# Rearranged places at the two ends of an expert loop: the overflow branch behind the first gathers, rows, norm factors and first weights in other buffers

## The chip, the cores and the metric

The kernel runs on one core of a Trainium2 chip. The metric is the device time of one execution in microseconds (us); smaller is better. The core has a matrix engine (PE, with its weight loads shown as PEld), a vector engine (DVE), a scalar engine (ACT), a general engine (POOL) and a queue engine (SP) that only issues DMAs here. Each works through its own list of instructions in order; they meet through semaphores, and each DMA queue is fed in the order in which its engine reaches the issuing instruction.

## What is computed

Two transformer blocks on 512 tokens of width 1024, in 32-bit floats. The first block ends with a mixture of 64 experts, and its layer norm; the second begins with an RMS norm and a projection.

```python
def first_block(...):                 # mixer, cross-attention, then
    ff = moe_ffn(x, w_router, router_bias, w_exp_gu, w_exp_down, w_sh_gu, w_sh_down)
    x = layer_norm(DEEPNORM_ALPHA * x + ff, ln3_g, ln3_b)
    return x

def moe_ffn(x2d, ...):                # each token goes to 8 of 64 experts, weights w
    ...
    out = swiglu(x2d[tok], w_exp_gu[e], w_exp_down[e]) * w      # summed into the token's row
    return routed + swiglu(x2d, w_sh_gu, w_sh_down)             # plus a shared expert

def second_block(x, norm_mix_w, w_in, ...):
    h = rmsnorm(x, norm_mix_w)
    z = h @ w_in
    ...
```

## The kernel before, in words

**Products.** Every float matrix is split into a rounded part and a remainder (`hi`, `lo`: line 118 on ACT, line 119 on DVE or, where asked for, POOL), and a product is three matmuls (`mm3`, lines 176 to 178).

**Places.** Tiles come from pools. A pool closed and another opened at the same addresses share memory, tile by tile: the later tile's first writer waits for the last user of whatever lay there. The left and the right side of memory are two stacks. In the expert stage the right side holds 32 KB of expert weights (`whl1`, slots 2 and 3 of `wtiles`) and then a ring of 7 raw weight places of 8 KB (`wraw`); the left side holds four `xt` places, a pool `mc` (with the gather buffers `gx[0]` to `gx[2]`), another 32 KB of expert weights (`whl0`, slots 0 and 1) and the loop's small tiles. The second block puts its transposed input `hT` where `whl1` was, its weight pool `w3` (3 raw places, 4 pairs of hi and lo, `wvg`) where `wraw` was, and on the left the big tiles `oB0`, `oB1`, `QSa`, `QSb`, `KH`, `KL` and a pool `nrm`.

**Order.** The order on each engine is fixed at build time by a planner that takes the instructions by priority (their order in the text) as its own estimate of the times finds them ready. So an instruction may be moved ahead of others that stand before it in the text. `issue_after(ins)` puts what is in its block behind `ins` on `ins`'s engine. A branch (`tc.If`, line 1363) is one unit on every engine: nothing is moved into it, but work is placed on either side of it.

**The start of the expert stage** (`moe`, from line 1396). `slot_steps` (lines 1250 to 1281) turns the router's choice into the list of rows of each expert, for four experts at a time: one-hot compares on DVE, small matmuls into the bank `lg`, casts on DVE. `load(i)` issues the three raw weight loads of expert i (3 MB). `moe_overflow` (line 1355) handles experts with more than 96 rows in a branch that is skipped here: each engine loads the largest count into a register (line 1362) and branches. It names two slots of `wtiles`, two `xt` places, one raw place and `gx[0]`. Then `fetch(i)` gathers the rows of expert i into `gx[i % 3]` by an indirect DMA on POOL (line 1287), `weights(i)` splits its weights and issues `load(i + 2)`, `rows(i)` transposes the gathered rows (line 1296) and splits them to `gT`, and `gated(i)` multiplies. `wtiles` hands out four slots in turn; the shared expert's weights are in slots 0 to 2. The branch takes slots 3 and 0, expert 0 slots 1 and 2.

**The end of the expert stage.** Each expert's result rows are scattered to a table in memory with 8 slots a token (plus one for the shared expert), except for the last two experts, whose rows are held and added by one-hot matmuls (line 1576). After the loop the first weights of the next block are loaded into freed expert weight places (`pre`, lines 1532 to 1535). The table is read back, per token tile t (128 tokens): `x3[t]` (slot 8) and four parts `(t, j)` of 1 MB, two slots each. Six parts of tiles 0 and 1, and later two more, go to the raw ring (`ring`); DVE adds some (`add_v`, line 1585), PE adds others through identity matmuls (`add_t`, lines 1595 and 1598). `ln3` loads the norm's factors `ln3g`, `ln3b` (line 257), reads the parts of tiles 2 and 3, and gives the functions for the norm.

**The start of the second block** (`block2`, line 1723). `begin` splits the first weights from `pre` into `w3` (ACT and POOL). `normed(t)` is the layer norm and the RMS norm of tile t (ACT 283, DVE 288 and 289, ACT 1648, DVE 1651 giving `hn`); for t = 0 it is queued behind `cast`, the last split on ACT. The loop over t transposes `hn` (line 299), multiplies by the two first weights, and behind tile 1 adds the rows of tiles 2 and 3 (`rows_v` on DVE, `rows_t` on PE).

Of the kernel before, what the change touches and what calls it, by code (L numbers as in the profile page):

```python
# [53 lines left out]
class Net:  # L54
# [1228 lines left out]
    def gather(self, gx, idx, pool, x2d, bufs=2):  # L1283
# [6 lines left out]
        gT = [pool.tile([P, KD, C], R, tag=f"gT{i}", name=self.name("gT"), bufs=bufs) for i in range(2)]  # L1290

        def turn(*halves):
# [62 lines left out]
    def moe_overflow(self, rk, vals, cnt, iota, gx, table, x2d, wge, wde):  # L1355

        nc, tc = self.nc, self.tc
        C = self.CAP
        wgu = [self.wtiles(4, 512) for _ in range(2)]
        wdn = [self.xt().rearrange("p (c n) -> p c n", c=2) for _ in range(2)]  # L1360
        raw = self.wrp.tile([P, self.RCH], F, tag="raw", name=self.name("raw"), bufs=self.nraw)
        most = nc.values_load(cnt[0:1, 64:65], min_val=0, max_val=S)
        with tc.If(most > C):
            with tc.For_i(0, 64, 1) as i:
                with tc.tile_pool(name="ov", bufs=1) as op_:
# [10 lines left out]
                    for b in range(1, -(-S // C)):  # L1376
# [4 lines left out]
                        gT = self.gather(gx, idx, op_, x2d, 1)()  # L1381
                        self.scatter(self.turn_rows(self.gated(gT, wgu, op_), op_), row, w, wdn, table, gx)

    def moe(self, x2, xT, lg):
# [75 lines left out]
        load(0)  # L1460
        load(1)
        self.moe_overflow(rk, vals, cnt, iota, gx[0], table, x2d[:, :], wge, wde)
        ep_s, ep = self.pool("ex")

# [4 lines left out]
        def fetch(i):  # L1469
            if i < E:  # L1470
                turn[i] = self.gather(gx[i % 3], sel(i)[0], ep, x2d[:, :])

        def rows(i, *halves):
            if i < E:
                gTs[i] = turn[i](*halves)
# [9 lines left out]

        fetch(0)
        fetch(1)
        weights(0)
        rows(0)
# [46 lines left out]
        y = self.wrp.tile([P, 2 * D], R, tag="raw", name=self.name("y"), bufs=self.nraw)  # L1536
        held[E - 2] = self.gx(1, R, C), self.gx(2, R, C)
        held[E - 1] = y[:C, :D], y[:C, D:]
# [7 lines left out]
        ring = lambda: self.wrp.tile([P, self.RCH], F, tag="raw", name=self.name("row"), bufs=self.nraw)  # L1546
        for t in range(2):
            nc.sync.dma_start(x3[:, t], self.table[t * P:(t + 1) * P, 8])
            for j in ((4, 6, 0, 2) if t == 0 else (0, 2)):
                read(t, j, ring())  # L1550
            if t == 0:
                for u in (2, 3):
                    nc.sync.dma_start(x3[:, u], self.table[u * P:(u + 1) * P, 8])
        turned(E - 2)
        back(E - 2)
        sgs[E - 1] = self.gated(gTs.pop(E - 1), wgs.pop(E - 1), ep)
# [10 lines left out]
        for j in (4, 6):  # L1567
            read(1, j, ring())
# [545 lines left out]
```

## Time and profile before

| | before |
|---|---|
| median of 3 runs | 2040.82 us (2033.28 to 2041.1) |
| the profiled execution, its own time | 2029.93 us |
| span of the profile | 2027.9 us |
| PE, DVE, ACT, POOL busy, share of the span | 91%, 68%, 51%, 24% |
| expert loop, first to last full pass | 615 to 1248 us |
| first matmul of the second block | 1325 us |

The profiled execution's own time is 2.0 us over its span, and 10.9 us under the median of the runs. Times in the rows below are microseconds from the start of the span. A row of a timeline gives start, duration, engine, line, operation, what it writes and reads, how often, and in brackets how long the engine stood idle before it and what released it. PE's busy time includes pipelining, so a PE that is busy all of a stretch is near, not at, its limit.

### The profile page before, as it was taken

The numbers are of one execution on the slowest core, as the hardware profiler recorded it, in microseconds if no ns is written. First come the engines' busy times: TensorE is split into PE (matmuls) and PEld (weight loads), VectorE is DVE, ScalarE is ACT, GpSimd is POOL, SyncE is SP. The second block draws the span as 40 slices with busy tenths as digits, with TensorE's granted clock in tenths as the row PEclk, the third lists the DMA queues.
The fourth block names the chain that finished last, engine by engine and source line by source line (L and its number), as shares of the span: only waits on it lengthen the run. The fifth ranks groups of instructions, "written<-read, shape, count | busy, mean of one in ns | idle before, by whom it ended". The sixth has DMA issues, their size and how long they took to land. (4 is left out here: it accounts for less than half of the span.)

```text
span 2027.9 us, 25347 instructions
## 1 busy us (share of the span) xinstructions
PE 1835.7 (91%) x9051; PEld 1407.0 (69%) x9051; DVE 1385.8 (68%) x2427; ACT 1037.6 (51%) x1522; POOL 483.4 (24%) x463
## 2 busy tenths in 40 slices
PE   6699899898979999998999898569999789999998
PEld 6477677686756776666766666248767578888886
DVE  8966677678788989887988887475576573333333
ACT  3363555336227878777877786124466542222220
POOL 6733111210432233432333442310033310000000
PEclk8899999899989999999999999789999899999999
DMA  5233323744339999999999998724210243333311
GB/s 144 63 85 104 115 63 117 246 154 143 146 142 340 365 356 361 351 350 339 365 359 362 350 359 293 292 111 128 65 53 1 84 125 95 102 94 95 103 52 42
DMA packets 178682, 381.00 MB, mean 188 GB/s; under 512 B 19749, under 2 KB 115313, under 8 KB 151929
## 3 DMA queue, kind: packets, MB, share of 16 engines
q1 hardware_dynamic: 156912, 327.54, 47.6%
q0 software_dynamic: 18784, 48.31, 7.0%
q10 hardware_dynamic: 2856, 3.49, 0.6%
q8 instruction: 73, 1.20, 0.2%
q14 instruction: 57, 0.46, 0.1%
HBM read 354.61 MB, written 41.16 MB: 195 GB/s over the span
## 5 line engine op out<-in xcount | busy, mean ns | idle before, releaser
L119 DVE TENSOR_TENSOR wlo<-raw,whi 128x1024 fp32r<-128x1024 f32 (+3 forms) x281 | 478.5, 1707 | 208.2 <-ACT whi L118 199.5
L118 ACT CAST whi<-raw 128x1024 fp32r<-128x1024 f32 (+3 forms) x288 | 406.2, 1415 | 407.6 <-PE acc L177 195.0
L177 PE MATMUL acc<-wlo,gT 128*96 128x512 f32 x512 | 207.5, 405 | 22.7 <-DVE wlo L119 22.3
L176 PE MATMUL acc<-whi,gT 128*96 128x512 f32 x512 | 215.9, 422 | 1.5 <-ACT whi L118 1.4
L1352 POOL DMA_INDIRECT table<-y,rowi x62 | 131.9, 2127 | 357.6 <-ACT aT L118 90.3
L178 PE MATMUL acc<-whi,gT 128*96 128x512 f32 x512 | 203.3, 397 | 0.0
L119 DVE TENSOR_TENSOR xt<-raw,xt 128x2048 fp32r<-128x2048 f32 x64 | 146.4, 2287 | 22.3 <-ACT xt L118 21.4
L176 PE MATMUL acc<-h3T,whi 128*128 128x512 f32 (+2 forms) x368 | 140.5, 382 | 0.2 <-ACT h3T L118 0.2
L177 PE MATMUL acc<-h3T,whi 128*128 128x512 f32 (+2 forms) x368 | 140.4, 382 | 0.1
L178 PE MATMUL acc<-h3T,wlo 128*128 128x512 f32 (+2 forms) x368 | 140.5, 382 | 0.0
L118 ACT CAST xt<-raw 128x2048 fp32r<-128x2048 f32 x64 | 122.1, 1908 | 14.7 <-DMA raw<-in_w_exp_down_dram 7.7
L177 PEld LDWEIGHTS acc<-wlo,gT 128*96 128x96 f32 x512 | 84.5, 165 | 55.0 <-DVE wlo L119 34.1
L1287 POOL DMA_INDIRECT gx<-x2d,idx x64 | 92.3, 1442 | 83.5 <-PE tr L1296 54.8
L178 PEld LDWEIGHTS acc<-whi,gT 128*96 128x96 f32 x512 | 83.7, 163 | 32.8 <-DVE gT L119 0.3
L176 PEld LDWEIGHTS acc<-whi,gT 128*96 128x96 f32 x512 | 85.8, 168 | 24.5 <-ACT whi L118 2.4
L176 PE MATMUL acc<-xt,aT 128*96 128x512 f32 x256 | 101.4, 396 | 1.0 <-ACT aT L118 1.0
L178 PE MATMUL acc<-xt,aT 128*96 128x512 f32 x256 | 100.6, 394 | 1.7 <-DVE aT L119 1.5
L177 PE MATMUL acc<-xt,aT 128*96 128x512 f32 x256 | 101.2, 395 | 0.0
L1349 ACT ACTIVATE y<-acc,wsl 96x512 f32<-96x512 f32 x124 | 83.6, 680 | 7.4 <-PE acc L178 7.1
L118 ACT CAST gT<-tr 128x384 fp32r<-128x384 f32 x128 | 59.7, 477 | 37.8 <-PE tr L1296 31.1
L176 PEld LDWEIGHTS acc<-h3T,whi 128*128 128x128 f32 x368 | 69.1, 188 | 13.8 <-ACT h3T L118 0.7
L177 PEld LDWEIGHTS acc<-h3T,whi 128*128 128x128 f32 x368 | 69.1, 188 | 13.6 <-DVE h3T L119 0.4
(718 smaller groups left out, 4427.3 us busy)
## 6 DMA issues: line engine op xcount, KB each, us to landing
raw<-in_w_exp_gu_dram SPq DMA_DIRECT2D x128, 1024.0 KB, 18.6
raw<-in_w_exp_down_dram SPq DMA_DIRECT2D x64, 1024.0 KB, 18.5
raw<-in_w_in_dram SPq DMA_DIRECT2D x36, 512.0 KB, 4.3
raw<-in_w_gate_dram SPq DMA_DIRECT2D x22, 512.0 KB, 4.0
raw<-in_w_up_dram SPq DMA_DIRECT2D x22, 512.0 KB, 3.8
raw<-in_w_down_dram SPq DMA_DIRECT2D x22, 512.0 KB, 3.7
row<-table SPq DMA_DIRECT2D x8, 1024.0 KB, 11.7
gsp<-sg POOLq DMA_DIRECT2D x16, 256.0 KB, 2.4
```

The lines of the kernel that those rows point to most:

```text
L118: first = nc.scalar.copy(hi, src)
L119: return first, (eng or nc.vector).tensor_tensor(lo, src, hi.bitcast(F), op=OP.subtract)
L176: mm(out, l[0], r[0], start=start, stop=False)
L177: mm(out, l[0], r[1], start=False, stop=False)
L178: mm(out, l[1], r[0], start=False, stop=stop)
L1287: nc.gpsimd.indirect_dma_start(out=gx, out_offset=None, in_=x2d, in_offset=bass.IndirectOffsetOnAxis(ap=idx, axis=0), bounds_check=S - 1, ...
L1349: nc.scalar.activation(y[:, nb * 512:(nb + 1) * 512], ps, AF.Copy, scale=w)
L1352: nc.gpsimd.indirect_dma_start(out=table, out_offset=bass.IndirectOffsetOnAxis(ap=row, axis=0), in_=y, in_offset=None, bounds_check=S * se ...
```

## The change

It has two parts.

At the start of the stage the order in the text is now: loads of experts 0 and 1, gathers of experts 0 and 1, the places of the branch, the split of expert 0's weights, the branch, and the rest. The branch uses `gx[2]` in place of `gx[0]`. Expert 0's weights take slots 3 and 0, the branch slots 1 and 2, which `self.wslot -= 2` hands to expert 1 again. The tiles `gT` are named when rows are transposed, not when they are gathered.

At the end of the stage the parts of tiles 0 and 1 are no longer read into the raw ring. Three go to the last expert's weight places (`spare`), the fourth of which holds the last expert's rows `y`; others go to `xt` places, and `(1, 6)` to a place of the second block. The reads stand behind `gated` of the last expert in the text. DVE adds one part more of tile 1, PE one less. The three rows of factors (`ln3_g`, `ln3_b`, `norm_mix_w`) go to the three raw places of `w3`, loaded before `begin`, where they were in the pool `nrm`, which now has an 8 KB place `row` for a part. The norm of tile 0 is no longer queued behind `cast`.

```diff
-        gT = [pool.tile([P, KD, C], R, tag=f"gT{i}", name=self.name("gT"), bufs=bufs) for i in range(2)]
-
-        def turn(*halves):
+        gT = []
+
+        def turn(pool, bufs, *halves):
+            if not gT:
+                gT.extend(pool.tile([P, KD, C], R, tag=f"gT{i}", name=self.name("gT"), bufs=bufs) for i in range(2))
...
         wgu = [self.wtiles(4, 512) for _ in range(2)]
-        wdn = [self.xt().rearrange("p (c n) -> p c n", c=2) for _ in range(2)]
-        raw = self.wrp.tile([P, self.RCH], F, tag="raw", name=self.name("raw"), bufs=self.nraw)
+        self.wslot -= 2
         most = nc.values_load(cnt[0:1, 64:65], min_val=0, max_val=S)
...
-        load(0)
-        load(1)
-        self.moe_overflow(rk, vals, cnt, iota, gx[0], table, x2d[:, :], wge, wde)
-        ep_s, ep = self.pool("ex")
...
+        load(0)
+        load(1)
         fetch(0)
         fetch(1)
+        places = ([self.xt().rearrange("p (c n) -> p c n", c=2) for _ in range(2)],
+                  self.wrp.tile([P, self.RCH], F, tag="raw", name=self.name("raw"), bufs=self.nraw))
         weights(0)
+        self.moe_overflow(rk, vals, cnt, iota, gx[2], table, x2d[:, :], wge, wde, *places)
+        ep_s, ep = self.pool("ex")
         rows(0)
...
-        y = self.wrp.tile([P, 2 * D], R, tag="raw", name=self.name("y"), bufs=self.nraw)
         held[E - 2] = self.gx(1, R, C), self.gx(2, R, C)
+        turned(E - 2)
+        back(E - 2)
+        sgs[E - 1] = self.gated(gTs.pop(E - 1), wgs.pop(E - 1), ep)
+
+        *spare, y = [fl(t) for _ in range(2) for t in self.wtiles(4, 512)]
         held[E - 1] = y[:C, :D], y[:C, D:]
...
-        ring = lambda: self.wrp.tile([P, self.RCH], F, tag="raw", name=self.name("row"), bufs=self.nraw)
-        for t in range(2):
+        def first(t):
             nc.sync.dma_start(x3[:, t], self.table[t * P:(t + 1) * P, 8])
-            for j in ((4, 6, 0, 2) if t == 0 else (0, 2)):
-                read(t, j, ring())
-            if t == 0:
-                for u in (2, 3):
-                    nc.sync.dma_start(x3[:, u], self.table[u * P:(u + 1) * P, 8])
-        turned(E - 2)
-        back(E - 2)
-        sgs[E - 1] = self.gated(gTs.pop(E - 1), wgs.pop(E - 1), ep)
+
+        first(0)
+        for j, tile in zip((0, 2, 4), spare):
+            read(0, j, tile.bitcast(F))
+        read(0, 6, self.xt().bitcast(F))
+        for t in range(1, NT):
+            first(t)
+        read(1, 0, self.xt().bitcast(F))
...
-        for j in (4, 6):
-            read(1, j, ring())
+        for j in (2, 4):
+            read(1, j, self.xt().bitcast(F))
...
-            add_v(1, (0, 2))
-            add_t(1, (4, 6))
+            add_v(1, (0, 2, 4))
...
-        def ln3(pool, places):
-            g, b = (self.row(pool, a[f"ln3_{x}"][0], D, f"ln3{x}", nc.sync) for x in "gb")
-            for t, j in ((2, 0), (2, 2), (2, 4), (2, 6), (3, 0), (3, 2)):
+        def ln3(pool, gains, places):
+            for t, j in ((1, 6), (2, 0), (2, 2), (2, 4), (2, 6), (3, 0), (3, 2)):
                 read(t, j, places.pop(0)())
+            add_t(1, (6,))
...
+        gains = []
+        for n in ("ln3_g", "ln3_b", "norm_mix_w_2"):
+            src = a[n][0]
+            gains.append(w1.tile([P, D], F, tag="raw", name=self.name("gain"), bufs=3))
+            nc.sync.dma_start(gains[-1], bass.AP(tensor=src.tensor, offset=src.offset, ap=[[0, P], [1, D]]))
+        gw = gains.pop()
...
-        gw = self.row(gp, A("norm_mix_w")[0], D, "gmix", nc.sync)
-
-        norm, rows_v, rows_t = pre(gp, [oB0, oB1, QSa, QSb, KHt, KLt, oB0, oB1])
+
+        row = lambda: gp.tile([P, 4 * S], F, tag="row", name=self.name("row"), bufs=1)
+        norm, rows_v, rows_t = pre(gp, gains, [QSb, KHt, KLt, row, oB0, oB1, QSa, QSb, KHt])
...
-        with tc.high_priority(), tc.issue_after(cast.ins):
+        with tc.high_priority():
             hs[0] = normed(0)
```

## Rows read from the trace of the kernel before

**Rows 1.** Busy time by stretch: PE, PEld, DVE, ACT, POOL, clock, DMA share, GB/s.
```profile
615.30:1248.00 632.70, 602.44 (x3078) 426.34 (x3077) 550.01 (x611) 501.27 (x558) 217.67 (x123) 0.99 0.98 353
1262.80:1300.60 37.80, 31.19 (x88) 16.51 (x86) 18.39 (x31) 3.74 (x6) 0.55 (x1) 0.91 0.94 375
1300.60:1323.40 22.80, 0.01 (x2) 0.01 (x1) 6.83 (x26) 6.75 (x9) 16.55 (x14) 0.58 0.53 198
```
**Rows 2.** The branch's line: count, duration ns min/median/max, first and last start.
```profile
L1363 PEldq COMPARE_BRANCH  x1: 4603/4603/4603, 596.2 to 596.2; - x1
L1363 DVEq EVENT_SEMAPHORE  x1: 21/21/21, 604.0 to 604.0; - x1
```
**Rows 3.** Timeline of POOL about the branch: the first and the third gather.
```profile
591.06 2.11 POOL L1287 DMA_INDIRECT gx<-x2d,idx  x1 [8.13 <-issue]
...
605.88 1.28 POOL L1287 DMA_INDIRECT gx<-x2d,idx  x1 [6.02 <-PE lg L1265]
```
**Rows 4.** Timeline of PE from the branch to expert 0.
```profile
604.07 0.81 PE L1265 MATMUL lg<-vals,oh 128*96 128x7 bf16 x8 [5.64 <-DVEq L1363]
...
613.43 2.15 PE L1296 MATMUL tr<-ident,gx 96*128 96x96 f32 x12 [7.28 <-DMA gx<-x2d,idx]
615.29 0.72 PE L176 MATMUL acc<-whi,gT 128*96 128x512 f32 x1
```
**Rows 5.** Timelines of ACT and DVE: splits of expert 0's weights, one on each.
```profile
598.36 1.90 ACT L118 CAST whi<-raw 128x2048 fp32r<-128x2048 f32 x1 [7.86 <-PE acc L178]
...
606.86 2.28 DVE L119 TENSOR_TENSOR xt<-raw,xt 128x2048 fp32r<-128x2048 f32 x1
```
**Rows 6.** Timeline of PE at the join: end of tile 0's additions, next transposes.
```profile
1282.30 1.88 PE L1598 MATMUL acc<-x,ident 128*128 128x512 f32 x4
...
1323.40 1.97 PE L299 MATMUL tr<-ident,hn 128*128 128x128 f32 x8 [22.79 <-DVE hn L1651]
```
**Rows 7.** Timelines of ACT, POOL and SP at the join: first weights and a factor.
```profile
1298.92 1.04 ACT L118 CAST whi<-whi 128x1024 fp32r<-128x1024 f32 x1 [30.27 <-PE acc L1595]
...
1304.77 1.44 ACT L283 ACTIVATE x<-acc,ve,rs 128x512 f32<-128x512 f32 x2
...
1300.06 4.66 POOL L119 TENSOR_TENSOR wlo<-whi,whi 128x1024 fp32r<-128x1024 f32 x2 [44.47 <-ACT whi L118]
...
1310.79 0.43 SPq L257 DMA_DIRECT2D ln3g<-in_ln_g_dram  x1
```
**Rows 8.** Timeline of DVE at the join: statistics, scaling and `hn` of tile 0.
```profile
1287.04 1.29 DVE L268 BATCH_NORM_STATS2 bnst<-acc 128x6 f32<-128x512 f32 x2
...
1290.58 0.16 DVE L273 SCALAR_TENSOR_TENSOR ve<-bnmv,rs 128x1 f32<-128x1 f32 x1
...
1315.64 1.22 DVE L288 TENSOR_TENSOR x<-x,ln3g 128x1024 f32<-128x1024 f32 x1 [13.86 <-DMA ln3g<-in_ln_g_dram]
1317.53 1.23 DVE L289 TENSOR_TENSOR x<-x,ln3b 128x1024 f32<-128x1024 f32 x1 [0.67 <-DMA ln3b<-in_ln_b_dram]
...
1322.06 1.28 DVE L1651 SCALAR_TENSOR_TENSOR hn<-x,rs,gmix 128x1024 f32<-128x1024 f32 x1
```
**Rows 9.** DVE's timeline, first addition of tile 2; critical chain, tile 2's first matmul.
```profile
1337.87 3.73 DVE L1585 TENSOR_TENSOR x<-x,oB 128x1024 f32<-128x1024 f32 x3
...
1368.95 0.60 PE acc L176
```
**Rows 10.** DVE's timeline behind the norms; DMA issues of the page, median landing last.
```profile
1376.17 1.29 DVE L1651 SCALAR_TENSOR_TENSOR hn<-x,rs,gmix 128x1024 f32<-128x1024 f32 x1
...
1386.60 1.22 DVE L119 TENSOR_TENSOR wlo<-raw,whi 128x1024 fp32r<-128x1024 f32 x1 [1.08 <-ACT whi L118]
...
raw<-in_w_in_dram SPq DMA_DIRECT2D x36, 512.0 KB, 4.3
```
**Rows 11.** Timelines of POOL and DVE: the same addition alone, and side by side.
```profile
1326.60 0.73 POOL L289 TENSOR_TENSOR x<-x,ln3b 128x256 f32<-128x256 f32 x1
...
1360.31 1.36 DVE L289 TENSOR_TENSOR x<-x,ln3b 128x768 f32<-128x768 f32 x1
...
1360.93 1.32 POOL L289 TENSOR_TENSOR x<-x,ln3b 128x256 f32<-128x256 f32 x1
```

More of the change, by code (lines that the diff above doesn't have):

```diff
@@ L1281, in slot_steps, with gather @@
         yield idx, w, f, row
-    def gather(self, gx, idx, pool, x2d, bufs=2):
+    def gather(self, gx, idx, x2d):
         nc = self.nc
@@ L1353, in scatter, with moe_overflow @@
                                      in_offset=None, bounds_check=S * self.TR - 1, oob_is_err=False)
-    def moe_overflow(self, rk, vals, cnt, iota, gx, table, x2d, wge, wde):
+    def moe_overflow(self, rk, vals, cnt, iota, gx, table, x2d, wge, wde, wdn, raw):
         nc, tc = self.nc, self.tc
@@ L1380, in moe_overflow @@
                                                     nc.vector)
-                        gT = self.gather(gx, idx, op_, x2d, 1)()
+                        gT = self.gather(gx, idx, x2d)(op_, 1)
                         self.scatter(self.turn_rows(self.gated(gT, wgu, op_), op_), row, w, wdn, table, gx)
@@ L1470, in fetch @@
             if i < E:
-                turn[i] = self.gather(gx[i % 3], sel(i)[0], ep, x2d[:, :])
+                turn[i] = self.gather(gx[i % 3], sel(i)[0], x2d[:, :])
         def rows(i, *halves):
             if i < E:
-                gTs[i] = turn[i](*halves)
+                gTs[i] = turn[i](ep, 2, *halves)
         def weights(i):
@@ L1616, in moe @@
         self.xts.close()
-        def ln3(pool, places):
-            g, b = (self.row(pool, a[f"ln3_{x}"][0], D, f"ln3{x}", nc.sync) for x in "gb")
-            for t, j in ((2, 0), (2, 2), (2, 4), (2, 6), (3, 0), (3, 2)):
+        def ln3(pool, gains, places):
+            for t, j in ((1, 6), (2, 0), (2, 2), (2, 4), (2, 6), (3, 0), (3, 2)):
                 read(t, j, places.pop(0)())
+            add_t(1, (6,))
             def norm(t):
-                self.layer_norm(x3[:, t], g, b, x3[:, t], pool, 256 if t else 0, banks=banks.pop(t))
+                self.layer_norm(x3[:, t], *gains, x3[:, t], pool, 256 if t else 0, banks=banks.pop(t))
             def rows_v(behind):
@@ L1745, in begin @@
             for r, ks in zip(first[0], (slice(0, 7), slice(7, 8))):
-                cast = self.split(r, wv[0][:, ks], wv[1][:, ks], eng=nc.gpsimd)[0]
-            return wu, cast
-        wu, cast = begin()
+                self.split(r, wv[0][:, ks], wv[1][:, ks], eng=nc.gpsimd)
+            return wu
+        wu = begin()
         obs, ob = self.pool("oB")
```

## The prediction, made before the change was built

> **What bounds the kernel now.** I read the busy time by stretch first, to find where PE stands idle, and then the timelines of all engines around each idle stretch. Through the expert loop PE is busy 602 of 633 us, and the DMA engines are occupied 98% of that time [rows 1]: nothing there is to be had for free. PE is idle at both ends of the loop. Ahead of it, PE waits 7.3 us for a gather and begins expert 0 at 615.29 [rows 4]. Behind it PE stands still for a whole stretch of 22.8 us [rows 1], until `hn` of tile 0 comes at 1323.4 [rows 6]. These two places are what the change touches.
>
> **The head: what is late there.** The planner already moved two gathers ahead of the branch: one starts at 591.06, another behind it, and the third at 605.88 [rows 3]. The third is expert 0's: before, the branch names `gx[0]`, so only the gather into that buffer has to stay behind it. PE's transposes start at 613.43, 7.55 after that issue, released by its landing [rows 3, 4].
>
> With `gx[2]` in the branch, expert 0's gather takes the first place, 591.06, and with the same 7.55 it lands at 598.6. That is ahead of the branch. Next in line is then the branch itself: the transposes and the splits to `gT` stay behind it in the text, because their pool opens there. PE leaves its own branch at 596.2 + 4.6 = 600.8, DVE passes at 604.0 [rows 2], and the first matmul behind the branch, at 604.07, waited for DVE's pass [rows 4]. So the transposes could start at 604.07, a gain of 613.43 - 604.07 = 9.4.
>
> What is added ahead of the branch on DVE: all three splits of expert 0's weights stand before it now, of which one, 2.28 us, was behind it [rows 5]. Without cover it puts DVE's pass at 606.3, a gain of 7.1. Something may pay it back. Before, ACT's second weight cast waited 7.9 us for PE, to 598.36 [rows 5], since slot 2 held the shared expert's down weights. Expert 0 now has slot 3, which nobody used, and slot 0, which is free earlier; so DVE can take these splits in gaps. I take 7.5, near the lower of the two. The gather moved behind the branch instead is that of expert 2, needed only one expert later; issued at 605.88 it lands at 613.4, about where expert 1's products would begin (606.3 + 1.9 + some 6), so it is the next thing to be late, by little. Raw places come free with the splits, so the weight loads move up with them, which a loop at 98% DMA needs if it is to keep the gain.
>
> From below: the branch cost PE 4.6 us [rows 2]. If ACT or DVE, whose skipped code now lies elsewhere, paid as much, DVE's pass moves to 610.9 and the gain is 613.43 - 610.9 = 2.5. So the head gives 2.5 to 9.4, taken 7.5.
>
> A rule that speaks against moving the branch is in the Trainium skill, Runtime: NRT & Kernel Launch, section Instruction fetch mechanics: a taken branch whose target is outside the fetched window stalls until the target page is fetched. The trace agrees for PE, with 4.6 us; by that rule for a second engine the sum would have 2.5 here in place of 7.5.
>
> **The join: what is late there.** The chain back from 1323.4 has these links. The gains `ln3g` are issued at 1310.79 and DVE's scaling waits 13.9 us for them, to 1315.64 [rows 7, 8]. They come so late because their pool lies over the raw first weights, which POOL reads until its fourth `wlo` split is over; POOL starts at 1300.06, behind ACT's first cast at 1298.92, which waited 30.3 us for PE's additions out of the raw ring [rows 7], where the pool `w3` lies. ACT's scaling of tile 0 stands behind all casts, at 1304.77 [rows 7], although its statistics were over at 1290.74 [rows 8].
>
> After the change no part is read into the raw ring, so `w3` is free when the last expert's weights are split, before 1262.8, where the additions' stretch begins. The casts and POOL's splits (at most the 16.6 us that POOL was busy in the idle stretch [rows 1]) can then run beside the additions, in which ACT was busy 3.7 of 37.8 us and POOL 0.6 [rows 1]: hidden. The gains go to `w3`'s raw places and are issued about then: hidden too, if SP puts them ahead of the reads or between them. If that cover were gone, their price is the 13.9 us of that wait.
>
> What is late next is PE's and DVE's own work on tile 0. PE has tile 0's sums at 1282.30 + 1.88 = 1284.2 [rows 6]; that hangs on the held experts' matmuls before it and isn't moved. Then: at most one addition on DVE in the way, 3.73 / 3 = 1.24 [rows 9]; statistics to shift, 1290.74 - 1287.04 = 3.7 [rows 8]; ACT's scaling, 1.44 [rows 7]; from the scaling by the gain to PE's transposes 1323.40 - 1315.64 less the 0.67 waited for `ln3b`, 7.1 [rows 6, 8]. Sum: 1284.2 + 1.2 + 3.7 + 1.4 + 7.1 = 1297.6, against 1323.4: a gain of 25.8.
>
> DVE gets one part more of tile 1 (two additions, 2.5 us) and PE one less (eight matmuls at 1.88 / 4 = 0.47, 3.8 us); both lie beside tile 0's chain. The bad end: part (1, 6) needs a place that comes free only when DVE has added (1, 0). If DVE does that behind `hn` of tile 0, and PE's order has (1, 6) ahead of the transposes, these start at 1297.6 + 2.5 (two additions) + 2.8 (1 MB at 375 GB/s [rows 1]) + 12 x 0.47 = 1308.5: a gain of 14.9. So the join gives 14.9 to 25.8; I take 24, near the upper end, since DVE is idle for most of the time in which tile 1's parts arrive (busy 18.4 of 37.8 [rows 1]).
>
> Does it last? Tile 2's additions on DVE begin at 1337.87, 14.5 behind tile 0's transposes, queued behind tile 1's turn, and its first matmul comes 31.1 later, at 1368.95 [rows 9]. This second stall moves along as long as the parts are there. With a gain of 24 the additions begin at 1313.9. All reads but the last two (16 MB), with the gains (1.5 MB), are 17.5 MB, which from 1262.8 at 375 GB/s takes 48.9 us: landed by 1311.7, 2 us ahead. It is close, but only tile 3's parts come last, and they are wanted later still.
>
> The gains now hold all three raw places of `w3` until the last `hn`, 1376.17 + 1.29 [rows 10]; the next stage's raw weights were loaded early before. One takes 4.3 us to land, and DVE splits the first at 1386.60 [rows 10], 9 us behind that `hn`; two of the three places come free with the layer norm, earlier. So I cost this at nothing; two landings in a row that are not hidden would cost some 4.
>
> POOL's splits beside DVE's additions: the same small POOL addition took 0.73 us alone and 1.32 beside a DVE addition [rows 11]. The Trainium skill, SBUF — State Buffer, section on who interferes with whom, calls this an exclusive lock between the two: whoever is late is blocked whole. The trace agrees (0.6 us of blocking). By it, additions caught behind POOL's last splits of up to 4.66 / 2 = 2.3 us each would take some 3 us off the 24.
>
> **Sum.** 7.5 + 24 = 31.5. The profiled execution's 2029.93 gives 1998.4. It lies 10.9 under the median of the runs; against that median, 2040.82, the forecast is 2009.3, and I give 2009.
>
> **Rivals.**
> - *Only the join.* The change of the head does nothing, as two of three gathers were ahead of the branch anyway and DVE's pass, with a longer list before it and a dear branch, takes the gather's place as the last wait. For it: 604.07 to 610.9 for DVE's pass is mine, not a row. Against it: 7.3 us of PE's wait carry the gather's name. 2040.8 - 24 = 2017.
> - *The join half stopped,* by (1, 6) as above: 2040.8 - 7.5 - 14.9 = 2018.
> - *Tile 2 takes it back.* If the reads of tiles 2 and 3 stand on SP behind a read that waits for its place, tile 2 starts where it did and the join gives nothing: 2040.8 - 7.5 = 2033. For it: the margin of 2 us above. Against it: before, the additions waited for tile 1's turn, not for data.
> - *Slower: the loop's pace.* A pass of the loop takes 632.7 / 62 = 10.2 us with DMA at 98%. If the new order of the places costs each pass more than 0.5 us, the 31.5 are eaten, and from (31.5 + 10.2) / 62 = 0.67 the kernel is slower by more than 0.5%. A raw place of the seven lost to the ring is 1 MB less in flight, up to 3.0 us of cover at 353 GB/s; at 1 us a pass the time is 2009 + 62 = 2071. For it: the loop has no slack. Against it: the places of a pass only swap their numbers, and the branch gives its raw place back as before.
>
> **How the numbers follow.** Forecast 0.62; only the join 0.13; the join half stopped 0.08; tile 2 takes it back 0.12; slower 0.05. A measurement of this kernel can tell about 0.5%, 10 us. Faster by more is the first three, 0.83; within it 0.12; slower 0.05. The range: below, both upper ends, 35, off the lowest time that is shown, 2029.93: 1994. Above, 2028: it takes in the join alone and the half stopped join, each with 10 us of spread between runs.
>
> **What would show it.** Right: expert 0's gather ahead of the branch and its transposes within 3 us of DVE's pass; the first experts' loads earlier by as much; ACT's casts and POOL's splits of the first weights before 1290; no wait for the gains; tile 0's transposes some 24 us sooner after the last expert, and tile 2's first matmul still about 45 us behind them. Wrong: a branch of several us on DVE or ACT, a pass of the loop longer than 10.3 us, a wait of the additions for `row` or `KH`, or of the next stage's casts for raw weights.

## The result, and the profile of the changed kernel

| | before | after |
|---|---|---|
| time, median (us) | 2037.34 (2033.28 to 2041.10, 4 runs) | 2016.87 (2016.38 to 2017.64, 4 runs) |
| ratio, 95% interval | | 0.9900 (0.9875 to 0.9926) |
| profiled execution (us) | 2029.93, span 2027.9 | 2017.64, span 2015.9 |

The change takes 20 us (15 to 25) off the kernel; forecast were 31.5. The forecast time, 2009, lies 8 us under the median, inside the range. The profiled execution of the kernel before was shorter than any of its four timed runs, that of the changed kernel was the longest of its four: the two profiles lie only 12.3 us apart. So I compare distances inside an execution, not its clock times.

**The stretches.** Idle and busy time of the changed kernel, by stretch, to set against [rows 1] (columns as there):

```profile
609.40:1246.00 636.60, 605.49 (x3083) 429.54 (x3083) 552.59 (x616) 499.41 (x557) 224.73 (x122) 0.98 0.98 351
1260.60:1300.49 39.89, 28.00 (x81) 15.02 (x79) 31.54 (x46) 9.43 (x13) 18.44 (x13) 0.87 1.01 408
1300.49:1323.40 22.91, 19.27 (x96) 15.87 (x97) 14.96 (x37) 7.36 (x12) 2.84 (x2) 0.85 0.44 173
```

The loop is as full as before. The empty 22.8 us behind the additions are gone: POOL's 16.6 us of splits now lie among the additions, and PE works where it stood still.

**The head.** Timelines of POOL, PE, ACT, DVE and SP around the branch, against [rows 3 to 5]:

```profile
594.39 1.07 POOL L1287 DMA_INDIRECT gx<-x2d,idx  x1 [8.16 <-DVE wsl L1276]
596.46 1.11 POOL L1287 DMA_INDIRECT gx<-x2d,idx  x1 [0.30 <-issue]
...
600.61 0.34 PE L1265 MATMUL lg<-vals,oh 128*96 128x7 bf16 x4 [1.65 <-DVE oh L1262]
606.01 2.15 PE L1298 MATMUL tr<-ident,gx 96*128 96x96 f32 x12 [5.05 <-PEq L1365]
609.40 0.72 PE L176 MATMUL acc<-whi,gT 128*96 128x512 f32 x1
...
587.51 1.91 ACT L118 CAST whi<-raw 128x2048 fp32r<-128x2048 f32 x1 [5.06 <-PE acc L178]
...
605.88 1.90 ACT L118 CAST whi<-raw 128x2048 fp32r<-128x2048 f32 x1 [10.71 <-PEq L1365]
607.69 1.23 ACT L118 CAST gT<-tr 128x384 fp32r<-128x384 f32 x3
...
596.61 2.28 DVE L119 TENSOR_TENSOR wlo<-raw,whi 128x2048 fp32r<-128x2048 f32 x1
...
551.64 7.59 SPq L142 DMA_DIRECT2D raw<-in_w_exp_gu_dram  x2
568.38 0.33 SPq L142 DMA_DIRECT2D raw<-in_w_exp_down_dram  x1
603.87 8.16 SPq L142 DMA_DIRECT2D raw<-in_w_exp_gu_dram  x2
```

SP's timeline of the kernel before, behind the loads of experts 0 and 1:

```profile
592.25 10.69 SPq L142 DMA_DIRECT2D raw<-in_w_exp_gu_dram  x2
604.14 0.33 SPq L142 DMA_DIRECT2D raw<-in_w_exp_down_dram  x1
609.16 2.53 SPq L142 DMA_DIRECT2D raw<-in_w_exp_gu_dram  x2
```

The loads leave three to an expert, in order, and in both kernels the six of experts 0 and 1 are out by 547. So the rows at 551.64, 558.90 (the second of the pair) and 568.38 are expert 2's loads, which the kernel before issues from 592.25 on; the row at 603.87 is expert 3's first, in the kernel before the one at 609.16.

Both first gathers stand ahead of the branch, and no wait carries their name any more. PE's transposes now wait 5.05 us for PE's own branch. The branch's line in the changed kernel, against [rows 2] (duration in ns, first and last start):

```profile
L1365 ACTq COMPARE_BRANCH  x1: 45/45/45, 595.3 to 595.3; - x1
L1365 POOLq COMPARE_BRANCH  x1: 50/50/50, 600.9 to 600.9; - x1
L1365 PEldq COMPARE_BRANCH  x1: 4483/4483/4483, 601.2 to 601.2; - x1
L1365 DVEq COMPARE_BRANCH  x1: 72/72/72, 603.2 to 603.2; - x1
```

The branch is dear on PE alone, 4.48 us, and cheap on the others. All three splits of expert 0 stand ahead of it (on ACT at 553.65, 558.74 and 587.51, on DVE at 556.06, 566.02 and 596.61). The cast at 605.88 is the first of expert 1, whose slots the branch borrows; it waited 10.7 us for PE's end of the branch, and the casts of expert 0's `gT` stood behind it.

**The join.** Timelines of DVE, ACT, POOL, SP and PE around tile 0's norm, against [rows 6 to 8]:

```profile
1271.85 7.01 DVE L1591 TENSOR_TENSOR x<-x,wlo 128x1024 f32<-128x1024 f32 x2
...
1282.42 0.70 DVE L268 BATCH_NORM_STATS2 bnst<-acc 128x6 f32<-128x512 f32 x1 [1.76 <-PE acc L1604]
...
1285.09 1.22 DVE L1591 TENSOR_TENSOR x<-x,xt 128x1024 f32<-128x1024 f32 x1
...
1290.91 0.15 DVE L273 SCALAR_TENSOR_TENSOR ve<-bnmv,rs 128x1 f32<-128x1 f32 x1
1291.03 2.48 DVE L1591 TENSOR_TENSOR x<-x,xt 128x1024 f32<-128x1024 f32 x2
1293.43 1.22 DVE L288 TENSOR_TENSOR x<-x,gain 128x1024 f32<-128x1024 f32 x1
...
1299.15 1.28 DVE L1656 SCALAR_TENSOR_TENSOR hn<-x,rs,gain 128x1024 f32<-128x1024 f32 x1
...
1268.17 0.43 ACT L118 CAST wvg<-wlo 128x280 fp32r<-128x280 f32 x1
...
1276.03 1.75 POOL L119 TENSOR_TENSOR wvg<-wlo,wvg 128x280 fp32r<-128x280 f32 x1
...
1274.90 0.33 SPq L1745 DMA_DIRECT2D gain<-in_ln_g_dram  x1
...
1281.36 1.88 PE L1604 MATMUL acc<-x,ident 128*128 128x512 f32 x4
1291.26 6.20 PE L1601 MATMUL acc<-QSb,ident 128*128 128x512 f32 x8 [8.01 <-DMA QSb<-table]
...
1300.49 1.09 PE L299 MATMUL tr<-ident,hn 128*128 128x128 f32 x8 [1.32 <-DVE hn L1656]
```

ACT's casts are over at 1268.6 and POOL's splits at 1277.8; the gains are issued at 1274.90 and DVE's scaling at 1293.43 waits for nothing. The statistics, 3.7 us from the first of them to the shift before [rows 8], now take 8.6 (1282.42 to 1291.06), since four additions of tile 1 of 1.22 us each are run in their middle, and two more stand ahead of the gain.

**Behind the join.** Timelines of DVE and PE at tile 2, against [rows 9], then of SP and ACT in the next stage:

```profile
1317.46 2.47 DVE L1591 TENSOR_TENSOR x<-x,KH 128x1024 f32<-128x1024 f32 x2
...
1350.25 0.60 PE L176 MATMUL acc<-wvg,hT 128*128 128x280 f32 x1
...
1351.33 0.38 SPq L142 DMA_DIRECT2D raw<-in_gmlp_ws_dram  x1
...
1451.42 1.05 ACT L118 CAST whi<-raw 128x1024 fp32r<-128x1024 f32 x1 [1.67 <-DMA raw<-in_w_in_dram]
```

Tile 2's first product follows tile 0's transposes by 49.8 us instead of 45.6. The first raw weights of the next stage are issued at 1351, when the first of the gains leave their places, and a cast at 1451 waits 1.67 us for raw weights where, in the kernel before, it did not wait.

**A ruler for the experiments.** Five marks are taken from the timelines of every profile: the last logits matmul of the router (PE), the first held matmul, `hn` of tile 0 and of tile 3, and the first addition of the output projection (DVE). The first three distances cover the loop with its head, the join and tiles 0 to 3; the fourth the attention, the fifth the rest to the end of the span. All in us:

```
                    loop    join   tiles  attention  rest    sum    timed ratio (95%)
before             708.3    54.3    54.1    255.2   396.6  1468.4
before, again      709.3    54.0    54.3    255.1   396.7  1469.4   0.9989 (0.9971-1.0006)
head only          705.0    48.3    53.6    255.8   396.4  1459.1   0.9946 (0.9924-0.9967)
join only          711.4    32.5    60.2    260.3   397.8  1462.2   0.9934 (0.9911-0.9957)
after              702.9    33.6    59.3    259.7   397.7  1453.3   0.9900 (0.9875-0.9926)
after, again       703.8    33.6    59.5    259.8   397.7  1454.3   0.9901 (0.9876-0.9926)
before, no branch  699.7    55.1    54.5    257.3   398.0  1464.6   0.9983 (0.9970-0.9997)
after, no branch   701.5    32.5    59.0    260.5   398.3  1451.7   0.9875 (0.9853-0.9897)
before, slots      708.1    46.7    54.8    257.2   397.5  1464.2   0.9977 (0.9954-1.0001)
rows in the ring   701.4    44.9    58.2    259.4   397.5  1461.4   0.9962 (0.9946-0.9979)
cast first         708.4    33.6    58.5    259.8   397.8  1458.2
part (1,4) on PE   704.4    32.9    63.8    258.8   397.5  1457.5   0.9928 (0.9902-0.9955)
gains elsewhere    702.2    33.6    57.9    258.0   396.6  1448.3   0.9900 (0.9874-0.9926)
gains, raw place   703.2    33.6    58.8    258.1   397.0  1450.7   0.9907 (0.9890-0.9924)
```

The router's last matmul itself, at the end of code whose text no kernel changes, lay between 559.4 and 568.6 in these fourteen executions, with no order by kernel. That scatter is why clock times mislead, and it may be a good part of the spread of the timed runs. By the ruler the change is worth 1468.9 - 1453.8 = 15.1 us: 5.5 in the loop, 20.5 in the join, less 5.2 in the tiles, 4.6 in the attention and 1.1 behind it. The timed 20 (15 to 25) just agree. The ruler has one or two executions of each kernel, and its loops scatter by some us: of the join alone it makes 6.7, where the timed runs have 9 to 18.

### The profile page after: what moved, and what is told of

It is laid out like the page before. It is cut to its first block, busy times and chain, and to the rows that moved or that the text cites. A ratio compares the mean times of both kernels' runs of the same rounds, so it can differ in the third digit from the quotient of the medians.

```text
span 2015.9 us, 25337 instructions
## 1 busy us (share of the span) xinstructions
PE 1848.5 (92%) x9043; PEld 1417.4 (70%) x9043; DVE 1394.7 (69%) x2429; ACT 1035.0 (51%) x1522; POOL 501.6 (25%) x463
## 5 line engine op out<-in xcount | busy, mean ns | idle before, releaser
L176 PE MATMUL acc<-whi,gT 128*96 128x512 f32 x512 | 218.4, 427 | 0.9 <-ACT gT L118 0.8
L178 PE MATMUL acc<-whi,gT 128*96 128x512 f32 x512 | 205.6, 402 | 1.8 <-DVE gT L119 1.8
L1287 POOL DMA_INDIRECT gx<-x2d,idx x64 | 98.5, 1539 | 74.7 <-PE tr L1298 41.1
L119 DVE TENSOR_TENSOR gT<-tr,gT 128x384 fp32r<-128x384 f32 x128 | 67.1, 550 | 18.9 <-ACT gT L118 18.5
L177 PEld LDWEIGHTS acc<-h3T,whi 128*128 128x128 f32 x368 | 69.1, 188 | 13.5 <-DVE h3T L119 0.4
```

Of the source, the lines that this page charges most:

```text
L119: return first, (eng or nc.vector).tensor_tensor(lo, src, hi.bitcast(F), op=OP.subtract)
L176: mm(out, l[0], r[0], start=start, stop=False)
L177: mm(out, l[0], r[1], start=False, stop=False)
L178: mm(out, l[1], r[0], start=False, stop=stop)
L1287: nc.gpsimd.indirect_dma_start(out=gx, out_offset=None, in_=x2d, in_offset=bass.IndirectOffsetOnAxis(ap=idx, axis=0), bounds_check=S - 1, ...
```

## The experiments

**1. The kernel before, once more,** to learn what two profiles of one program differ by. No edit.

> The kernel before, unchanged, for a second profile of it. Theory A (the length of the unchanged attention stage differs between executions, and the profiled execution of before happened to be a short one): from the last addition of tile 3 to the end this profile is longer than before's by 4 to 10 us, with a lower granted clock from 1460 us on, and the span is 2033 to 2040. Theory B (the changed kernel itself loses 6.5 us behind tile 3): the stretch from tile 3 to the end has the same length as in the profile before, within 1.5 us.

The stretch from tile 3 to the projection was 255.1 again, against 255.2: theory A fell. The 4.6 us that the changed kernel loses there are its own. The loop with its head came out the same within 1 us, while the router's end was 1 us later.

**2 to 4. Each half alone, and both again.** The halves are the change's own hunks: the gathers, the branch and the order of weights, or everything from the last expert on.

> Only the head: the branch names gx[2] and stands behind the first two gathers and the first expert's weight splits; the join is as before. Theory of the prediction: the gather was the last wait, the gain is 7.5 us (2.5 to 9.4), a ratio of 0.9963. Theory from the trace of the changed kernel: PE's own branch, which moved with PE's work to 601.2 us, and the weight split that ended up behind it take the gather's place; PE starts expert 0 some 6 us sooner but works at half clock longer, the loads begin 11 us later, and at the end of the loop 2 us are left: ratio 0.999, not to be told from 1.

> Only the join: the parts of the rows, the gains and the first weights have their new places, no issue of the norm behind the last cast, part (1, 4) on DVE; the head is as before. Theory of the prediction: 24 us, ratio 0.9882, with tile 0's transposes 24 us after the last held matmul's old distance less. Theory from the trace of the changed kernel: 20.7 us at tile 0's transposes, 16.4 left at the end of tile 3, since DVE runs tile 1's additions in the middle of tile 0's statistics and tile 1 comes late: ratio 0.992.

> The changed kernel once more, beside the two halves on the same chip, so that their sum can be set against it. If the halves add up, its gain is that of the join alone and that of the head alone together: by the prediction 31.5 us (ratio 0.9845), by the trace 18 to 20 us (ratio 0.990 to 0.991).

The head alone gave 11 us (7 to 15), far more than the "2 us" that I had read from the two first profiles: there the changed kernel's router had ended 3 us later. In the loop it is 4 us; the other 6 are in the join, 48.3 instead of 54.2, in code that this kernel leaves alone. The join alone gave 13.5 (9 to 18): 21.7 at `hn` of tile 0, of which 11.1 are spent in the tiles and the attention. The halves don't add up: 5.9 and 21.7 in the join, each alone, make 20.5 together. The expected "loads begin 11 us later" was a misreading: as in the changed kernel, expert 2's loads leave some 40 us sooner here, and expert 3's first 8 us sooner.

**5. Why the head shortens the join.** The branch borrows two weight slots; the head gives them back, so all later weights, the next stage's first ones too, lie two slots further back. That bookkeeping line alone, in the kernel before:

```diff
         wgu = [self.wtiles(4, 512) for _ in range(2)]
+        self.wslot -= 2
```

> The kernel before, with one edit of the head alone: the branch gives its two weight slots back, so that all later weights, the first weights of the next stage too, lie two slots further back; branch and gathers stand as before. Theory A (the head moved the first weights to slots that part of the casts can be made from sooner, and that is where the 5.8 us of the head-only kernel in the join come from): from the first held matmul to hn of tile 0 about 48 us instead of 54, and the head itself no shorter (708 to 711 us from the router's last logits matmul to the first held matmul, or more, as expert 0 now shares its slots with the branch); ratio 0.997 to 0.998. Theory B (the join is shorter there because the loop ends sooner): 54 us as before, ratio 1.

The join took 46.7 us, the loop 708.1 as before: theory A holds (the timed ratio alone could not be told from 1). ACT's and SP's timelines show how: the first cast waits for DVE's additions only, no longer for PE's [rows 7], and the gain is issued 27.6 us behind the first held matmul (at 1275.15), instead of 43.0 (1310.79 [rows 7] less 1267.78):

```profile
1292.97 1.04 ACT L118 CAST whi<-whi 128x1024 fp32r<-128x1024 f32 x1 [16.93 <-DVE x L1586]
...
1302.74 0.34 SPq L257 DMA_DIRECT2D ln3g<-in_ln_g_dram  x1
```

**6. The rows back in the raw ring,** all else as in the changed kernel:

```diff
-        for j, tile in zip((0, 2, 4), spare):
-            read(0, j, tile.bitcast(F))
-        read(0, 6, self.xt().bitcast(F))
+        for j in (0, 2, 4, 6):
+            read(0, j, ring())
...
-        read(1, 0, self.xt().bitcast(F))
+        read(1, 0, ring())
...
-            read(1, j, self.xt().bitcast(F))
+            read(1, j, ring())
```

> The changed kernel, but the parts of tiles 0 and 1 that have new places go back into the raw ring, over which the next stage's pools lie. Theory of the prediction (the place of these parts is what held the casts of the first weights, POOL's splits and the gains): from the first held matmul to hn of tile 0 it is 46 to 54 us again, as with the head alone and in the kernel before, instead of 33.6; most of the join's gain is gone; ratio 0.993 to 0.997. Rival (the gains' place and the order of SP's reads carry it): 33 to 38 us, ratio 0.990.

The join took 44.9 us and 11.3 of its 20.5 were gone, just beyond the expected 46 to 54; the rival (33 to 38) falls. So the rows' places carry a little more than half; the slots carry 7, and, with the rows moved, add nothing (32.5 with the join alone, 33.6 with both). How they carry it I had not foreseen. POOL's and DVE's timelines of this kernel:

```profile
1294.19 6.54 POOL L119 TENSOR_TENSOR wlo<-whi,whi 128x1024 fp32r<-128x1024 f32 x2 [38.86 <-DMA gain<-in_ln_b_dram]
1300.69 4.66 POOL L119 TENSOR_TENSOR wlo<-wlo,whi 128x1024 fp32r<-128x1024 f32 x2
1305.29 4.33 POOL L119 TENSOR_TENSOR wvg<-whi,wvg 128x1960 fp32r<-128x1960 f32 x1
...
1295.26 3.26 DVE L289 TENSOR_TENSOR x<-x,gain 128x1024 f32<-128x1024 f32 x1
...
1300.52 0.15 DVE L244 TENSOR_SCALAR rs<-rs 128x1 int32<-128x1 int32 x1
1300.70 2.35 DVE L247 SCALAR_TENSOR_TENSOR rs<-rs,rs 128x1 f32<-128x1 f32 x1
1303.09 2.27 DVE L251 SCALAR_TENSOR_TENSOR rs<-rs,rs 128x1 f32<-128x1 f32 x1
1305.40 4.23 DVE L247 SCALAR_TENSOR_TENSOR rs<-rs,rs 128x1 f32<-128x1 f32 x1
...
1310.40 0.22 DVE L247 SCALAR_TENSOR_TENSOR rs<-rs,rs 128x1 f32<-128x1 f32 x1
```

It is no wait for a gain or a cast. Late in the ring, POOL's splits fall into the middle of the norm, and DVE's one-column steps, 0.16 to 0.22 us elsewhere (1310.40, when POOL was done), take as long as a whole split of POOL each: 2.35, 2.27 and 4.23. With line 289, 3.26 instead of 1.23, and two small remainders this is 11.0 of the 11.3 us. The Trainium skill, SBUF — State Buffer, section Who interferes with whom, says that a DVE instruction with two SBUF inputs shares a port with a POOL instruction that reads SBUF, and that the later one is blocked whole. The trace agrees to the step: line 244, with one input, took 0.15 beside the split that ran to 1300.7.

**7, 8. The branch left out** of the kernel before and of the changed one:

```diff
-        most = nc.values_load(cnt[0:1, 64:65], min_val=0, max_val=S)
-        with tc.If(most > C):
...
```

> The kernel before with the overflow branch left out (the code for experts with more than 96 rows isn't there; for this input it is skipped anyway). Theory A (the gather behind the branch, and then PE's own branch, are what expert 0 waits for): expert 0's transposes start within 2 us of PE's last slot matmul, and from the router's last logits matmul to the first held matmul it is 7 to 10 us shorter than the 708 to 711 us with the branch; ratio 0.995 to 0.9965. Theory B (neither matters, the loop runs at the pace of the weight loads whatever its start): the distance stays at 706 or more, ratio 0.998 to 1.

> The changed kernel with the overflow branch left out in the same way. Theory A (in the changed kernel PE's branch, 4.5 us, and the weight split that stands behind it are what is left of the head's loss): from the router's last logits matmul to the first held matmul 3 to 5 us less than the changed kernel's 703 to 704 us, ratio against the kernel before 0.987 to 0.989. Theory B (the branch is hidden there): no difference, 0.990.

Without it the loop of the kernel before is 9.1 us shorter, as theory A expected, with expert 0's first product 7 us sooner. The theory's other sign failed: the transposes started 4.0 us behind the slot matmuls, 3.6 of them a wait for the gather, which without the branch is still the last to come. The timed gain, 0.0017 (3.5 us), is less than expected: the join and what follows came out longer by 5 us. The edit leaves every place where it was; only the planner's order around them can have moved. In the changed kernel expert 0 starts another 7 us sooner (transposes 36.4 instead of 43.4 behind the router), but the loop ends only 1.9 sooner, under the expected 3 to 5, though the timed ratio, 0.9875, is inside the expected range. So the branch does cost the start of expert 0 some 7 us; the changed kernel's loop hands on little of it, that of the kernel before all of it, and why they differ is open. One sign is in line 142, the weight loads: how long ACT's casts waited for them in the loop (total us, times), in the kernel before,

```profile
  ACT whi L118: 43.6, 45
```

in the changed one,

```profile
  ACT whi L118: 72.1, 62
```

and in the changed one without the branch:

```profile
  ACT whi L118: 87.5, 70
```

In the last of them PE stood idle for 41.9 us from expert 0's first product to the first held matmul, against 33.9 and 37.2 in the changed kernel's two profiles, and expert 10's first load left 110.2 us behind the router's end, against 110.9 and 110.7: what PE gains at the start it waits for in the loop, as the loads come hardly sooner. It isn't the whole answer, as the casts of the kernel before without the branch waited 78.9.

**9. The norm behind the last cast again,** `issue_after(cast.ins)` restored around tile 0's norm.

> The changed kernel with the norm of tile 0 issued behind the last cast of the first weights again. Both theories: the casts end at 1268, before the first sums at 1282, so that this part of the change is worth nothing; hn of tile 0 at 33.6 us behind the first held matmul, span within 5 us of the changed kernel's. If the planner orders ACT or DVE otherwise because of it, hn comes up to 2.5 us later or sooner.

The join took 33.6, to the tenth: this part of the change is worth nothing once the casts end at 1268. The span, 2022.7, lies 6.8 over the changed kernel's first profile, more than the expected 5; 1.9 of it stood before the router's end and 5.5 in the loop, and the changed kernel's second profile was as long, 2022.9.

**10. Part (1, 4) back on PE:**

```diff
-            add_v(1, (0, 2, 4))
+            add_v(1, (0, 2))
...
-            add_t(1, (6,))
+            add_t(1, (4, 6))
```

> The changed kernel, but part (1, 4) of tile 1 is added on PE again, as before the change: two additions less on DVE, eight matmuls more on PE. Theory of the prediction (DVE's extra part lies beside tile 0's chain): no gain, tile 0's transposes 34.9 us behind the first held matmul as in the changed kernel. Theory of the trace (all of tile 1's additions are run in the middle of tile 0's statistics): hn of tile 0 comes 2.5 us sooner, but the transposes only 1 us sooner, since PE's queue has the late part (1, 6) ahead of them; ratio 0.990.

Tile 0's transposes came 0.7 us sooner, near the trace's 1, but so did its `hn`, where 2.5 were expected. And tile 1 lost 7.8: `hn` of tile 1 follows that of tile 0 by 21.6 us instead of 13.7. PE's timeline shows why: the planner put tile 1's last part behind tile 0's transposes, while in the changed kernel PE does it in the time in which it waits for `hn` anyway.

```profile
1304.65 1.97 PE L299 MATMUL tr<-ident,hn 128*128 128x128 f32 x8 [11.57 <-DVE hn L1656]
1308.46 3.59 PE L1601 MATMUL acc<-QSb,ident 128*128 128x512 f32 x8
```

**11. The gains elsewhere,** in the place of a later part, so that the three raw places are free:

```diff
-        for n in ("ln3_g", "ln3_b", "norm_mix_w_2"):
-            gains.append(w1.tile([P, D], F, tag="raw", ...))
+        both = QSb()
+        gains = [both[:, :D], both[:, D:]]
+        gw = gp.tile([P, D], F, name="gmix")
...
-        norm, rows_v, rows_t = pre(gp, gains, [QSb, KHt, KLt, row, oB0, oB1, QSa, QSb, KHt])
+        norm, rows_v, rows_t = pre(gp, gains, [KHt, KLt, row, oB0, oB1, QSa, KHt, KLt, row])
```

> The changed kernel, but the norm's two gains lie in the place of QSb and the third gain in the norm's own pool, so that the three raw places of the next stage's weights are free from the start; the later parts of the rows move on by one place. Theory A (holding the three raw places makes the next stage's loads late, which costs the 4.6 us that are lost between tile 3's norm and the output projection, and the 1 us behind it): from tile 3's norm to the first addition of the output projection 255 to 256 us again instead of 259.7, ratio against before 0.9875. Theory B (the loss lies in the order in which the planner put the attention's work): the distance stays at 259 or more, ratio 0.990. If the gains come late to tile 0 in their new place, tile 0's transposes are later by what DVE's scaling then waits for them.

SP's timeline: the next stage's raw weights are issued 1.8 us behind the start of tile 0's `hn`, instead of 52.2 (1351.33 less 1299.15), and the cast that waited at 1451.42 does not wait here.

```profile
1303.79 0.43 SPq L142 DMA_DIRECT2D raw<-in_gmlp_ws_dram  x1
1304.27 3.94 SPq L142 DMA_DIRECT2D raw<-in_w_in_dram  x2
```

From `hn` of tile 0 to the end it is 712.5 us instead of 716.8 and 716.9: the gains' place costs some 4.3, of which 1.5 lie in the tiles, 1.7 in the attention and 1.1 behind it. The next kernel, which has the same edit, gets 713.9, which makes it 2.9. The attention took 258.0, between the two theories: 1.7 of its 4.6 are the raw places'. Two kernels that hold no gains there lie at 257.3 and 257.2 (before without the branch, before with the slots moved), so that some 2 us come and go with the order that the planner finds; how is open. The join is 33.6 as in the changed kernel, so it isn't the gains' place in `w3` that carries the join. By the clock the 5 us over the changed kernel could not be told (0.9900 against 0.9900 and 0.9901).

**12. The branch's raw place.** As 11, and the branch takes its raw buffer from its own pool, so that the ring keeps all seven:

```diff
+                    raw = op_.tile([P, 1024], F, name="rawov")
...
-        places = ([self.xt()...], self.wrp.tile([P, self.RCH], F, tag="raw", ...))
+        places = [self.xt()...]
```

> The changed kernel with two edits: the gains lie elsewhere, as in the kernel named gains_elsewhere (in QSb's place and in the norm's pool), and the branch takes its raw place in a pool of its own behind the test, so that the ring has all seven places for expert weights from the start. Theory A (the loop is bound by the weight loads, and what starts them sooner counts): the first load of expert 2 is issued some 25 us sooner, 1 MB more is there at the loop's start, and from the router's last logits matmul to the first held matmul it is 2 to 4 us less than 702 to 704; together with the other edit 7 to 8 us under the changed kernel, ratio 0.986 to 0.987. Theory B (PE's start of expert 0 behind its branch sets the loop's end): 702 to 704 as in the changed kernel, ratio 0.988.

The premise failed: expert 2's loads needed no help, as they leave 11.0 and 3.7 us ahead of the router's end and 5.7 behind it in the changed kernel, and here too. The next load, expert 3's first, left 37.9 us behind the router's end instead of 41.3 (43.1 in the kernel of 11). SP's waits around the branch say what held it, in the changed kernel,

```profile
SPq L142 <- DVEq L1365: 13.2, 1, 13.2
```

and here (total, times, longest):

```profile
SPq L1364 <- DVE oh L1262: 22.6, 1, 22.6
SPq L142 <- DVE wlo L119: 8.8, 1, 8.8
```

In the changed kernel it waits for DVE to pass the branch. Here SP stands at the branch's test for 22.6 us, to 590.3, and then 8.8 more for DVE's last split of expert 0, which frees a raw place. So the raw place lent to the branch cost that load 3 to 5 us, and the test cost it nothing that the split would not have. The loop took 703.2 all the same, but PE's branch was longer here, 5.70 us, and expert 0's first product came at 49.6 instead of 46.8 (48.7 in the kernel of 11), so the run doesn't tell the theories apart. With 0.9907 the kernel is no better than the changed one by the clock. A version in which all loads are sooner was not tried.

## Why the prediction came out as it did

**The diagnosis was right.** PE's two idle places were what the change touched, and the gathers, the casts, the splits and the gains left the path as forecast.

**The head: 7.5 forecast, 5.4 measured** (loop with head 709.3, mean of four with the old head, against 703.9, mean of eight with the new one; single profiles scatter by 7). It is inside the bounds, by two errors that made up for each other. The start was sooner than my best case: behind the router's end, expert 0's transposes came at 43.4 instead of 54.0, 10.6 sooner, where "the transposes could start at 604.07, a gain of 9.4" was to be the most. DVE's pass was not put off to 606.3. All three splits of expert 0 stood ahead of it, but two of them ran about the router's end, at 556 and 566, "in gaps" as I had thought possible but not priced. So the pass came at 41.2 (603.8) instead of 44.6, and what was late next was PE's own branch, which ended at 43.1 (605.7). I had dropped it from the list by its 600.8, or 41.3; with DVE's split now ahead of `oh`, the last slot matmuls waited 1.65 for DVE, and PE reached its branch 1.8 later.

"The weight loads move up with them" came true at first: expert 2's three loads left 44, 47 and 39 us sooner behind the router's end, expert 3's first 8.5 (41.3 instead of 49.8). Expert 0's first product came 9.0 sooner (46.8 instead of 55.9). But the lead did not last, and the sum had taken a lead at the start as a gain at the end. Expert 10's first load left 7.2 sooner, the last load of the loop 4.9 (means of two profiles each), and of the 9.0 the loop kept 5.4. Part of the rest is PE's clock: in the first 7.6 us of expert 0 the granted clock was 0.50 and 0.65 in the two profiles of the changed kernel (0.50 is the lower level, 1.2 GHz) and it did 21 and 26 matmuls; before, it was 0.80 and 0.75, and 32 and 30. PE had stood still ahead of it in both. What else shrinks the lead of the loads is open.

The rule on taken branches that I had set against the head (the Trainium skill, Runtime: NRT & Kernel Launch, Instruction fetch mechanics) made the sum 2.5 if a second engine paid. None did: 45 to 72 ns on ACT, POOL and DVE, and PE alone paid, as before.

**The join: 24 forecast, 20.5 at `hn` of tile 0.** Two terms of its sum were mis-sized. Tile 0's sums came 1.3 us later behind the first held matmul (15.8 instead of 14.5): the third held matmul now waited 1.23 for DVE's last evacuation, where before none of the first seven waited. (The evacuation itself stood only 0.14 later, behind a cast on ACT that had moved up.) And "at most one addition on DVE in the way, 1.24" were six, 7.4, of which ACT's scaling, 1.4, ran beside two. POOL's splits did slow the additions beside them (7.01 us for two that take 2.48 alone), but that cost nothing, as PE's last sum, 1281.36, was later than DVE's part of it, 1278.9.

**"Does it last?" failed.** 10.9 of the 20.5 were given back. In the tiles, 5.2: (1, 6) did hold PE, 8.0 us, as the half-stopped rival had it; tile 0's transposes did not wait for it, but tile 1's sums did, and its `hn` came 3.5 later behind tile 0's than before (that (1, 6) is the reason is read from the order of the rows; no run moves it alone). Tiles 2 and 3 added 1.7. In the attention and behind it, 5.7. "I cost this at nothing" was the raw places of the next stage, with 4 named as the price if two landings were not hidden. Giving those places back returned 4.3 and 2.9 in the two kernels that do it, the tiles' 1.5 among the first, so that the value taken was wrong. That the price comes near is in part luck: the one landing that shows was not beside the norms, where I looked, but 90 us later, at 1451, and took 1.67. The other half of the 5.7 is not the raw places'.

**The rivals.** "Only the join" named 2017, the time that came out, by luck: the head does work, and the join kept some 10 of its 24. "Tile 2 takes it back" named a loss of which a quarter came, by another way: tile 2's additions waited for no read (1317.46), they stood behind tile 1's turn, as before. The loop's pace changed little: from expert 0's first product to the first held matmul it is 652.5 and 653.4 before, 656.1 and 656.9 after, with the start 9 sooner; that is 0.06 us a pass, where the rival needed 0.5.

**What stays open.** The 5 us between the ruler's 15.1 and the timed 20, within its interval (both profiles of the kernel before were shorter than, or the shortest of, their timed runs, both of the changed kernel the longest of theirs); the some 2 us of the attention's loss that kernels without the gains' edit show too.

## What to carry to other kernels

A wait that is removed from a join is worth what is left at the next stage, so cost the buffers that the new places keep until then: here the gains' places took 3 to 4 us back, part of it 90 us later. In a stage that runs at the pace of its loads, follow a sooner start to the stage's end before counting it: here 9 us at the first expert were 5 at the last. A buffer that is lent to a branch is not free until the engines have passed it, though the body is skipped: here a load and a cast waited 13.2 and 10.7 us for that. Before two kernels are compared by one profile each, measure the change between marks inside the execution; here the end of the router, behind unchanged code, varied by 9 us, more than most of the effects.

## What the runs showed of the hardware

A DVE step on one column, 0.16 to 0.22 us alone, took 2.27 to 4.23 us beside POOL's splits when it had two inputs, and 0.15 when it had one: of all that ran beside POOL here, a chain of such steps lost the most. The branch, whose body is skipped, cost 4.48 us on PE and under 0.1 us on each of the other engines (4.60 on PE before [rows 2]); in the twelve profiles that have it, it took 4.17 to 5.70 us on PE.
